# Six of eleven inner tiles of a last projection as block products, with weight sums kept in DRAM

## The chip, the cores and the metric

The kernel runs on one core of a Trainium2 chip. The time is the device time of one execution in microseconds (us). A core has five engines with instruction queues of their own: TensorE (PE in the profile, with PEld for its weight loads), VectorE (DVE), ScalarE (ACT), GpSimd (POOL) and SyncE (SP), which here only issues transfers. Data are worked on in SBUF, a memory of 128 partitions; TensorE writes its sums to PSUM, and everything else lies in DRAM (HBM).

## The reference, cut to what matters

One block of a streaming encoder on 512 tokens of 1,024 features: a normalised input, one combined projection, attention (A) and a gated recurrence (B) side by side, both merged into `h`, then a gated feed-forward part and a last normalisation.

```python
h = h + (g_a * ya + g_b * yb) @ w_o[l]
hn = rmsnorm(h, norm_ffn_g[l])
gu = hn @ w_ffn_in[l]                       # 1024 -> 2 x 2816
g, up = jnp.split(gu, 2, axis=-1)
h = h + (jax.nn.silu(g) * up) @ w_ffn_out[l]   # 2816 -> 1024: the last projection
...
return rmsnorm(h, final_norm_g)
```

The change is about the last projection: 512 tokens x 2,816 inner values x 1,024 outputs, all in float32.

## The kernel before, in words

**Precision.** Each float32 operand is split into a high part (ACT copies it to a shorter float type, line 82) and a low part (DVE subtracts the high part from the source, line 83). A product is then three matmuls (`mm3`, lines 76 to 78): high x high, high x low, low x high. Each loads one 128x128 block of the stationary operand and streams the other past it, 512 or 256 columns at a time.

**Order of stages.** Projections for the recurrence; the first head's queries and keys; the values of the first half of the heads (`v_tile`, line 643); the recurrence's output (`yb`, lines 742 to 747); sixteen heads of attention; its output (`ya`); `w_o` with the sum `h`; the feed-forward's input projection (`fg`, `fu`, lines 842 to 909); the last projection (lines 915 to 987).

**The planner.** The code is laid out by a planner that puts each engine's instructions in an order by its own estimate of when their inputs are ready. Inside `tc.manual_schedule(engines=...)` the named engines keep the order of the code. Before, this holds for PE in the attention heads, not in the last projection. Tiles come from pools: a tag has a number of slots (`bufs`), and an instruction that writes a new tile waits until the slot's earlier tile has been read for the last time. Pools on the left and the right of SBUF open and close in turn, and a new pool's tiles wait for the old tiles below them.

**Weights.** `plan` lists the weight chunks, `load` (line 140) issues their transfers from SP into `raw` tiles (three in the small pool `wp`), `prefetch` (line 220) splits them into `whl` tiles (four in `wp`), and `weights(name, ahead)` asks for a chunk and for the ones behind it.

**The input projection** already works with block products: for `fg` and `fu` from tile 2 on, weights and input are seen as 2x2 blocks, sums of weight blocks are built on DVE (`weight_sums`, line 164), and seven products of sums replace eight of blocks (`block_product`, line 277). The eleven activation tiles `act2[0..10]` (128 x 2 x 512: 256 inner values each, that is two inner tiles of 128 in the matmul's terms) lie in the pool `acp` of 13 slots.

**The last projection before.** The 22 inner blocks of 128 are taken in six chunks of four (`fo0_0` and so on), for the first 512 columns and then for the second. `split_act` splits each activation tile, on POOL for tiles 0, 1, 2 and 4 and on DVE for the rest. For the first half each chunk is applied to the four token tiles (128 tokens) in four PSUM tiles. For the second half four chunks go that way, and the last two are applied token tile by token tile, so that `h_out` (add to `h`, sum of squares, factor), `out_norm`, `h_norm` and the stores of one tile run beside the matmuls of the next. The last token tile is taken in two pieces of 256 columns, in all its chunks. The first half's `h_out` runs when that half is done, with the factor on POOL.

Of the kernel before, what the change touches and what calls it, by code (L numbers as in the profile page):

```python
# [14 lines left out]
P = 128  # L15
# [21 lines left out]
def block_kernel(ctx: ExitStack, tc: tile.TileContext, x, norm_mix_g, w_in, b_merge, rel_table,  # L37
# [700 lines left out]

    for t in range(NT):
        v_tile(0, t)  # L740

    for j in range(KT):
        if j == 6:
            prob = scores(0)
        po = mm_tile(f"po_yb{j}")
        project(po, weights(f"yb{j - j % 2}"), j % 2, rnn)
        dve.scalar_tensor_tensor(zB[j], zB[j], 1.0, po[:], ALU.add, ALU.mult)
# [131 lines left out]
    barrier[0] = "fo0_16"  # L879
# [11 lines left out]
    def split_act(i):  # L891
        o = act2[i]
        pl, bufs = (acp, 13) if i == 0 else (ohp, 6) if i < 7 else (op, 4)
        hi = pl.tile([P, 2, S], F32R, tag="act", bufs=bufs, name=f"act_hi{i}")
        lo = acp.tile([P, 2, S], F32R, tag="act", bufs=13, name=f"act_lo{i}")
        act.activation(hi[:], o[:], AF.Copy)  # L896
        (pool if i in (0, 1, 2, 4) else dve).tensor_sub(lo[:], o[:], f(hi[:]))  # L897
        for c in range(2):
            actT[2 * i + c] = (hi[:, c], lo[:, c])
# [16 lines left out]
    ohp = ctx.enter_context(pool_of("act_hi", 6, "right"))  # L916
    op = ctx.enter_context(pool_of("out", 4, "right"))
    for i, name in enumerate(n for n, *_rest in chunks if n.startswith("fo")):
        if i % 4 >= 2:
            extra[name] = op  # L920
    barrier[0] = None
# [3 lines left out]

    def out_tile(t, po, k0, wf, at):
        for k in range(min(4, FT - k0)):
            kk = k0 + k
            mm3(po[:, 0:at.stop - at.start], actT[kk][0][:, t * P:(t + 1) * P], actT[kk][1][:, t * P:(t + 1) * P],
                wf(0, k, at), wf(1, k, at), kk == 0, kk == FT - 1)  # L930
# [30 lines left out]
    ks = list(range(0, FT, 4))  # L961
    late = 4
    for cc, tags in enumerate(("mmmm", "sstmm")):

        pieces = [(t, every) for t in range(NT)] if cc == 0 else [*((t, every) for t in range(3)), (3, slice(0, CW)), (3, slice(CW, S))]
# [47 lines left out]
```

## Time and profile before

| | |
|---|---|
| runs without profiler, median of 3 | 877.0 us (876.93 to 877.12) |
| the profiled execution's own time | 877.08 us |
| its span, first to last instruction | 875.3 us |
| granted TensorE clock, mean | 0.998 |
| transfers | 90.08 MB, mean 103 GB/s |
| largest groups | L76, L77, L78 on `po_out`: 198 matmuls each |
| whl_fo splits on DVE (L83) | 22, 27.8 us |
| whl_fo splits on ACT (L82) | 22, 23.0 us |

The profile is of one execution. Its page gives busy times, the span in 40 slices, the chain of waits that ended last, and groups of instructions by line, engine, operation and tile; "x198 | 72.5, 366 | 0.0" means 198 instructions, 72.5 us busy, 366 ns each on average, and 0.0 us of idle time on their engine just before them, with the releaser behind it. In the timeline a row is start, length, engine, line, operation, tiles, shape and count. Lines L76 to L83 are those of helpers, so groups are told apart by their tiles: `po_out` is the last projection, `p_fu` and `q_fu` the input projection, `yb` the recurrence's output.

### The profile page before, as it was taken

How to read it: one execution, taken by the hardware profiler on the slowest of the kernel's cores; microseconds unless marked ns; L12 is line 12 of the kernel's file. 1: busy time of each engine (PE TensorE's matmuls, PEld its weight loads, DVE VectorE, ACT ScalarE, POOL GpSimd, SP SyncE). 2: the span in 40 equal slices, each digit the busy share in tenths (PEclk: the TensorE clock that was granted, in tenths of full speed). 3: DMA queues.
4: the chain of work that ended last, by engine and by line, in shares of the span. 5: the costliest groups of instructions: out<-in, count | busy, mean ns of one | idle time of the engine just before them, and what ended most of it. 6: DMA issues, size and time to landing. Idle time of an engine off the chain costs nothing.

```text
span 875.3 us, 12954 instructions
## 1 busy us (share of the span) xinstructions
PE 864.5 (99%) x5028; PEld 760.0 (87%) x5028; DVE 545.9 (62%) x850; ACT 479.7 (55%) x830; POOL 104.2 (12%) x138
## 2 busy tenths in 40 slices
PE   8999999999999999999999999999999999999997
PEld 6977887888888888888888889999999999888886
DVE  5786776543646656566557457888887886644203
ACT  6588687531456656566534367565555654823103
POOL 2022221200122222233000000000000001301100
PEclk9999999999999999999999999999999999999999
DMA  8332334323532222242224531433333332453002
GB/s 268 94 90 84 96 95 122 98 92 100 141 113 72 62 76 81 73 121 64 94 96 151 186 97 41 144 100 104 97 116 101 118 101 78 136 171 121 25 1 97
DMA packets 84030, 90.08 MB, mean 103 GB/s; under 512 B 5376, under 2 KB 70512, under 8 KB 83968
## 3 DMA queue, kind: packets, MB, share of 16 engines
q1 hardware_dynamic: 80288, 81.58, 29.9%
q10 hardware_dynamic: 3680, 7.67, 3.0%
q8 instruction: 39, 0.64, 0.3%
q14 instruction: 23, 0.19, 0.1%
HBM read 87.10 MB, written 2.14 MB: 102 GB/s over the span
## 4 chain that ended last, share of the span: by engine, by line
PE 97%; ACT 1%; DVE 1%; DMA 0%; issue 0%; ACTq 0%
PE po_out L76 5%; PE po_out L78 5%; PE po_out L77 5%; PE p_fg L76 2%; PE o L713 2%; PE p_fg L77 2%; PE p_fg L78 2%; PE p_fu L78 2%; PE p_fu L77 2%; PE p_fu L76 2%; PE pT L693 2%; PE po_gb L77 2%; PE po_gb L76 2%; PE po_ga L76 2%; PE po_v L76 2%; PE po_ga L78 2%
## 5 line engine op out<-in xcount | busy, mean ns | idle before, releaser
L77 PE MATMUL po_out<-whl_fo,act_hi 128*128 128x512 f32 (+1 forms) x198 | 72.5, 366 | 0.0
L76 PE MATMUL po_out<-whl_fo,act_hi 128*128 128x512 f32 (+1 forms) x198 | 72.3, 366 | 0.0
L78 PE MATMUL po_out<-whl_fo,act_lo 128*128 128x512 f32 (+1 forms) x198 | 71.7, 365 | 0.0
L682 POOL TENSOR_SCALAR p<-p,rl 128x128 f32<-128x128 f32 (+1 forms) x64 | 39.6, 637 | 164.5 <-DVE rl L680 164.4
L83 DVE TENSOR_TENSOR whl_fo<-raw_fo,whl_fo 128x1024 fp32r<-128x1024 f32 x22 | 27.8, 1273 | 44.3 <-ACT whl_fo L82 43.9
L82 ACT ACTIVATE whl_fo<-raw_fo 128x1024 fp32r<-128x1024 f32 x22 | 23.0, 1057 | 49.0 <-PE po_out L78 36.8
L897 POOL TENSOR_TENSOR act_lo<-act,act_hi 128x1024 fp32r<-128x1024 f32 x4 | 10.9, 2716 | 323.5 <-ACT act_hi L896 321.4
L679 ACT ACTIVATE p<-p,m 128x128 f32<-128x128 f32 (+1 forms) x64 | 35.8, 562 | 12.7 <-DVE m L678 12.7
L78 PEld LDWEIGHTS po_out<-whl_fo,act_lo 128*128 128x128 f32 x198 | 37.3, 189 | 6.0
L77 PEld LDWEIGHTS po_out<-whl_fo,act_hi 128*128 128x128 f32 x198 | 37.4, 189 | 6.0
L76 PEld LDWEIGHTS po_out<-whl_fo,act_hi 128*128 128x128 f32 x198 | 37.4, 189 | 6.0
L83 DVE TENSOR_TENSOR pp<-pT,pp 128x384 fp32r<-128x384 f32 (+1 forms) x48 | 27.8, 595 | 9.8 <-ACT pp L82 9.7
L678 DVE CUSTOM_DVE_ANT_0 p<-s,bias 128x128 f32<-128x128 f32 (+1 forms) x64 | 29.2, 482 | 3.9 <-PE s L675 3.8
L83 DVE TENSOR_TENSOR whl_qk<-raw_qk,whl_qk 128x1024 fp32r<-128x1024 f32 x16 | 21.5, 1346 | 14.4 <-ACT whl_qk L82 14.3
L76 PE MATMUL po_gr<-xnT,whl_gr 128*128 128x512 f32 (+1 forms) x80 | 28.1, 352 | 0.1
L77 PE MATMUL po_xr<-xnT,whl_xr 128*128 128x512 f32 (+1 forms) x80 | 27.9, 354 | 0.0
L83 DVE TENSOR_TENSOR whl_fg_s<-s_fg,whl_fg_s 128x1024 fp32r<-128x1024 f32 x20 | 25.6, 1293 | 3.7 <-ACT whl_fg_s L82 3.7
L77 PE MATMUL po_gr<-xnT,whl_gr 128*128 128x512 f32 (+1 forms) x80 | 27.8, 348 | 0.0
L78 PE MATMUL po_gr<-xnT,whl_gr 128*128 128x512 f32 (+1 forms) x80 | 27.5, 348 | 0.0
L78 PE MATMUL po_xr<-xnT,whl_xr 128*128 128x512 f32 (+1 forms) x80 | 27.3, 346 | 0.0
L76 PE MATMUL po_xr<-xnT,whl_xr 128*128 128x512 f32 (+1 forms) x80 | 26.6, 351 | 0.6 <-ACT xnT L365 0.6
L83 DVE TENSOR_TENSOR whl_fu_s<-s_fu,whl_fu_s 128x1024 fp32r<-128x1024 f32 x20 | 24.0, 1220 | 4.5 <-ACT whl_fu_s L82 4.5
(336 smaller groups left out, 2984.5 us busy)
## 6 DMA issues: line engine op xcount, KB each, us to landing
raw_fg<-in_w_ffn_in_dram SPq DMA_DIRECT2D x24, 512.0 KB, 4.5
raw_fu<-in_w_ffn_in_dram SPq DMA_DIRECT2D x22, 512.0 KB, 3.8
raw_fo<-in_w_ffn_out_dram SPq DMA_DIRECT2D x22, 512.0 KB, 4.2
raw_qk<-in_w_in_dram SPq DMA_DIRECT2D x32, 256.0 KB, 3.3
raw_xr<-in_w_in_dram SPq DMA_DIRECT2D x8, 512.0 KB, 4.7
raw_gr<-in_w_in_dram SPq DMA_DIRECT2D x8, 512.0 KB, 3.6
raw_gb<-in_w_in_dram SPq DMA_DIRECT2D x8, 512.0 KB, 3.9
raw_v<-in_w_in_dram SPq DMA_DIRECT2D x8, 512.0 KB, 3.6
```

Of the source, the lines that this page charges most:

```text
L76: pe.matmul(o, sh, mh, start=start, stop=False, skip_group_check=parts)
L77: pe.matmul(o, sh, ml, start=False, stop=False, skip_group_check=parts)
L78: pe.matmul(o, sl, mh, start=False, stop=stop, skip_group_check=parts)
L82: act.activation(hi, src, AF.Copy)
L83: dve.tensor_sub(lo, src, f(hi))
L678: dve.tensor_tensor_reduce(prob[qb][:], scs[qb], bias[:, S - w:S], -1.0, 3e38, ALU.add, ALU.min, nmax[:, qb:qb + 1])
L679: act.activation(prob[qb][:], prob[qb][:], AF.Exp, bias=nmax[:, qb:qb + 1], scale=-1.0, accum_out=lsum[:, qb:qb + 1])
L682: pool.tensor_scalar(prob[qb][:], prob[qb][:], rl[:, qb:qb + 1], 1.0, ALU.mult, ALU.mult)
L693: pe.transpose(pt[:, at * P:(at + 1) * P], prob[qb][:, kb * P:(kb + 1) * P], ident[:])
L713: pe.matmul(po[:, S - n:S], st, pp[i][:, part, lo:lo + n], start=kb == 0 and part == 0, stop=kb == NT - 1 and part == 1)
L897: (pool if i in (0, 1, 2, 4) else dve).tensor_sub(lo[:], o[:], f(hi[:]))
```

## The change

Of the eleven inner tiles of 256, tiles 0, 1, 2 (front) and 9, 10 (tail) stay plain, and tiles 3 to 8 form three units of two, (3, 4), (5, 6), (7, 8). A unit is a product of 512 tokens x 512 inner values x 1,024 outputs, seen as 2x2 blocks of 256 tokens x 256 inner values and 256 inner values x 512 outputs, and is worked out with seven block products, for all three units together.

- **Weight sums.** `spill(u)` loads a unit's four weight blocks (512 KB each), forms four sums with four subtractions on DVE, and stores them to DRAM (`sums_d`). It stands ahead of the value tiles (unit 0) and at the first and the fourth `yb` output (units 1 and 2). It uses the four `pt` slots in `aw2` that the attention heads use later for their transposed probabilities (`pp`).
- **Parts.** `fo_part` loads one part (a plain weight block, or a sum out of DRAM), and splits it. There are 31 where there were 22 splits. The first two are asked for at the start of the last pass of the input projection, into the small pool; from there on they rotate over ten `whl` slots (four in `wp`, six in the new pool `op`) and seven raw slots (three and four).
- **Activations.** Front and tail tiles are split whole (tile 0 on POOL, the others on DVE). Of the units, seven half-size parts each are split (`act_part`); `act_sums` and `act_last_sum` form the sums on DVE, four per unit, the last two in place. The pool `op` has eight `act` slots.
- **Order.** The whole stage stands in `manual_schedule` for PE and DVE. All eight quarters (four token tiles x two column halves) have a PSUM tile at once. After the front tiles, five of them are added to `h`; those PSUM tiles then take products, which `read` adds to `h` where one product belongs to more than one quarter. The tail tiles are applied token tile by token tile, first to the left half, then to the right, with `h_out` and `h_norm` in between; only the last token tile's right half is in two pieces of 256 columns, and only for the tail.

The core of the diff:

```diff
-    for cc in range(2):
-        for k0 in range(0, FT, 4):
-            plan(f"fo{cc}_{k0}", cols(w_ffn_out, cc * S, S), rows=k0 * P, kts=min(4, FT - k0))
+    front, units, tail = (0, 1, 2), ((3, 4), (5, 6), (7, 8)), (9, 10)
...
+    def spill(u):
+        r = [aw2.tile([P, 2, S], F32, tag="pt", bufs=4, name=f"spill{u}_{n}") for n in range(4)]
+        for n in range(4):
+            sp.dma_start(out=r[n][:], in_=fo_block(units[u][n // 2], n % 2))
+        b11, b12, b21, b22 = (t[:] for t in r)
+        dve.tensor_sub(b11, b12, b11)
+        dve.tensor_sub(b12, b22, b12)
+        dve.tensor_sub(b22, b22, b11)
+        dve.tensor_sub(b21, b21, b22)
+        for n, i in enumerate((0, 3, 1, 2)):
+            sp.dma_start(out=sums_d[u][n][:], in_=r[i][:])
+
+    spill(0)
     for t in range(NT):
         v_tile(0, t)
+    SPILLS = (0, 3)
     for j in range(KT):
...
+        if j in SPILLS:
+            spill(SPILLS.index(j) + 1)
...
-        pl, bufs = (acp, 13) if i == 0 else (ohp, 6) if i < 7 else (op, 4)
+        pl, bufs = (op, 8) if i in front[1:] else (acp, 13)
...
-        (pool if i in (0, 1, 2, 4) else dve).tensor_sub(lo[:], o[:], f(hi[:]))
+        (pool if i == 0 else dve).tensor_sub(lo[:], o[:], f(hi[:]))
...
+    def fo_part(name, src):
+        raw_pl, bufs = raw_rooms[parts_made[0] % len(raw_rooms)]
+        raw = raw_pl.tile([P, 2, S], F32, tag="raw", bufs=bufs, name=f"raw_{name}")
+        sp.dma_start(out=raw[:], in_=src)
+        pl, tag, bufs = rooms[parts_made[0] % len(rooms)]
+        parts_made[0] += 1
+        hl = pl.tile([P, 2, 2, S], F32R, tag=tag, bufs=bufs, name=f"whl_{name}")
+        split_pair(hl, raw[:])
+        return hl
...
         if j == FT - 2:
             split_act(0)
+            for cc in range(2):
+                fo_plain(0, cc)
...
-    ohp = ctx.enter_context(pool_of("act_hi", 6, "right"))
     op = ctx.enter_context(pool_of("out", 4, "right"))
+    rooms[:] = [(wp, "whl", 4)] * 4 + [(op, "whl", 6)] * 6
+    raw_rooms[:] = [(wp, 3)] * 3 + [(op, 4)] * 4
...
+    def act_sums(u):
+        t = acp.tile([P, 2, 2, 256], F32, tag="act", bufs=13, name=f"s12_{u}")
+        s1, s2 = t[:, 0], t[:, 1]
+        a11, a21, a22 = (part_of(n, u) for n in ("a11", "a21", "a22"))
+        dve.tensor_add(s1, a21, a22)
+        dve.tensor_sub(s2, s1, a11)
+        dve.tensor_sub(a21, a11, a21)
...
+    def make(a, b):
+        for u in range(len(units)):
+            src = ...
+            parts_w[b, u] = fo_part(f"{b}_{u}", src)
+            act_part(a, u)
+
+    def multiply(a, b, half, cc, start):
+        for u in range(len(units)):
+            for i in range(2):
+                x, w = acts[a, u], parts_w[b, u]
+                tok = slice(i * P, (i + 1) * P)
+                for k in range(2):
+                    mm3(quarter[2 * half + i, cc][:], x[:, 0, k, tok], x[:, 1, k, tok], w[:, 0, k], w[:, 1, k],
+                        start and u == 0 and k == 0, u == len(units) - 1 and k == 1, parts=True)
...
+    with tc.manual_schedule(engines={mybir.EngineType.PE, mybir.EngineType.DVE}):
+        split_act(1)
+        fo_plain(1, 0)
+        fo_plain(1, 1)
+        for t, cc in everywhere:
+            plain_tile(front[0], t, cc, True)
+        split_act(2)
+        fo_plain(2, 0)
+        fo_plain(2, 1)
+        for t, cc in everywhere:
+            plain_tile(front[1], t, cc, False)
+        make("a11", "b11")
+        for u in every_unit:
+            act_sums(u)
+        for t, cc in ((2, 0), (3, 0), (0, 1), (1, 1), (3, 1), (0, 0), (1, 0), (2, 1)):
+            plain_tile(front[2], t, cc, False)
+        make("s1", "t1")
+        for t, cc in ((2, 0), (3, 0), (0, 1), (1, 1), (3, 1)):
+            add(t, cc)
+        make("s2", "t2")
+        multiply("a11", "b11", 1, 0, True)
+        read(1, 0, (0, 0))
+        multiply("s1", "t1", 0, 1, True)
+        make("a12", "b21")
+        read(0, 1, (1, 1))
+        for u in every_unit:
+            act_last_sum(u)
+        multiply("s2", "t2", 1, 0, False)
+        make("s3", "t3")
+        read(1, 0, (0, 1))
+        multiply("a12", "b21", 0, 0, False)
+        make("s4", "b22")
+        multiply("s3", "t3", 1, 0, False)
+        read(1, 0, (1, 1))
+        make("a22", "t4")
+        multiply("s4", "b22", 0, 1, False)
+        for i in tail:
+            split_act(i)
+            for cc in range(2):
+                fo_plain(i, cc)
+        multiply("a22", "t4", 1, 0, False)
+        for t in range(NT):
+            for i in tail:
+                plain_tile(i, t, 0, False)
+            h_out(0, t, quarter[t, 0], pool, 0, every)
...
+            for n, (po, at, start) in enumerate(pieces):
+                for i in tail:
+                    plain_tile(i, t, 1, start and i == tail[0], at, po[:, 0:at.stop - at.start])
+                if n == len(pieces) - 1:
+                    part = out_norm(t, n + 1)
+                h_out(1, t, po, dve, n + 1, at)
+            h_norm(t, part, n + 1)
```

More of the change, by code (lines that the diff above doesn't have):

```diff
@@ new lines, in block_kernel, with plain_tile, add @@
+    quarter = {(t, cc): pl.tile([P, S], F32, tag=tag, bufs=bufs, name=f"po_out{t}_{cc}") for (t, cc), (pl, tag, bufs) in c_tags.items()}
+    def plain_tile(i, t, cc, start, at=every, o=None):
+        hi, lo = actT[i]
+        w = plain[i, cc]
+        tok = slice(t * P, (t + 1) * P)
+        for k in range(2):
+            mm3(quarter[t, cc][:] if o is None else o, hi[:, k, tok], lo[:, k, tok], w[:, 0, k, at], w[:, 1, k, at],
+                start and k == 0, k == 1, parts=True)
+    def add(t, cc):
+        hs = ht[t][:, cc * S:(cc + 1) * S]
+        dve.tensor_add(hs, quarter[t, cc][:], hs)
```

86 lines of the change are left out of this document (46 added, 40 removed).

## The prediction

> **What bounds the kernel now.** I read the page first (busy shares, the chain that ended last), then busy time by stretches of the last projection, then PE's timeline there.
>
> ```profile
> span 875.3 us, 12954 instructions
> PE 864.5 (99%) x5028; PEld 760.0 (87%) x5028; DVE 545.9 (62%) x850; ACT 479.7 (55%) x830; POOL 104.2 (12%) x138
> PE 97%; ACT 1%; DVE 1%; DMA 0%; issue 0%; ACTq 0%
> ```
>
> ```profile
> 744.00:805.00 61.00, 61.00 (x287) 51.17 (x287) 29.73 (x26) 28.17 (x31) 8.46 (x3) 1.00 0.42 137
> 805.00:869.00 64.00, 64.00 (x345) 55.46 (x343) 15.53 (x28) 13.28 (x27) 6.02 (x4) 1.00 0.13 44
> ```
>
> Columns of the second view: the stretch and its length, then busy time of PE, PEld, DVE, ACT and POOL, the granted clock, the DMA share and GB/s. PE is busy in every microsecond of the stage that the change rewrites, at clock 1.00, while DVE and ACT are busy for half of its first part and a quarter of its second. The chain is PE for 97%. So a matmul taken out of this stage shortens the time by its step, as long as DVE, ACT and the loads keep up with a faster PE. A busy PE alone is no proof of pace, so the step is taken from start times:
>
> ```profile
> L76 PE MATMUL po_out<-whl_fo,act_hi x198: 277/389/396, 743.8 to 868.5; 128*128 128x512 f32 x154, 128*128 128x256 f32 x44
> L77 PE MATMUL po_out<-whl_fo,act_hi x198: 282/389/398, 744.1 to 868.6; 128*128 128x512 f32 x154, 128*128 128x256 f32 x44
> L78 PE MATMUL po_out<-whl_fo,act_lo x198: 279/389/397, 744.3 to 868.7; 128*128 128x512 f32 x154, 128*128 128x256 f32 x44
> ```
>
> ```profile
> 852.27 0.40 PE L76 MATMUL po_out<-whl_fo,act_hi 128*128 128x512 f32 x1
> ...
> 864.54 0.28 PE L76 MATMUL po_out<-whl_fo,act_hi 128*128 128x256 f32 x1
> ...
> 868.74 0.28 PE L78 MATMUL po_out<-whl_fo,act_lo 128*128 128x256 f32 x1
> ```
>
> The stage has 3 x 154 = 462 wide (512) and 3 x 44 = 132 narrow (256) matmuls. Between the first two timeline rows lie three token tiles of 18 wide ones: (864.54 - 852.27) / 54 = 0.227 us a step. Behind them 36 narrow ones: (868.74 - 864.54) / 35 = 0.120 us. The 389 ns that the view gives for one matmul is a pipelined length, not a step.
>
> **What PE saves.** After the change: the three front tiles are 3 inner tiles x 8 quarters x 2 x 3 = 144 wide matmuls; the seven products, over three units, two token tiles, two k and three parts, are 7 x 36 = 252; the two tail tiles are 84 wide and 24 narrow. Together 480 wide and 24 narrow. By the steps: before 462 x 0.227 + 132 x 0.120 = 120.7; after 480 x 0.227 + 24 x 0.120 = 111.8. PE's work falls by 8.9 us. Of that, about 8.2 (36 x 0.227) is the block product, seven products for eight; the rest is that 108 narrow matmuls become 54 wide ones (0.120 against 0.1135 for half a wide one).
>
> [...]
>
> **What DVE and ACT must now deliver.** Both PE and DVE run the new stage in the order of the code; ACT's order is still planned.
>
> ```profile
> L83 DVE TENSOR_TENSOR whl_fo<-raw_fo,whl_fo 128x1024 fp32r<-128x1024 f32 x20 | 25.3, 1278 | 43.7 <-ACT whl_fo L82 43.3
> L82 ACT ACTIVATE whl_fo<-raw_fo 128x1024 fp32r<-128x1024 f32 x20 | 20.9, 1058 | 49.0 <-PE po_out L78 36.8 <-DMA raw_fo<-in_w_ffn_out_dram 11.2 <-PE q_fu L78 1.0
> L936 DVE TENSOR_TENSOR h<-po_out,h 128x512 f32<-128x512 f32 (+1 forms) x8 | 5.1, 653 | 26.5 <-PE po_out L78 26.5
> ```
>
> ```profile
> 699.79 2.36 DVE L83 TENSOR_TENSOR whl_fg_s<-s_fg,whl_fg_s 128x1024 fp32r<-128x1024 f32 x2 [0.52 <-ACT whl_fg_s L82]
> 702.07 0.69 DVE L178 TENSOR_TENSOR s_fu<-raw_fu,raw_fu 128x512 f32<-128x512 f32 x1
> ...
> 703.27 0.68 DVE L179 TENSOR_TENSOR s_fu<-s_fu,raw_fu 128x512 f32<-128x512 f32 x1
> 733.39 0.62 ACT L82 ACTIVATE whl_fu_a<-raw_fu 128x512 fp32r<-128x512 f32 x1
> ```
>
> Back to back, DVE's step is (702.07 - 699.79) / 2 = 1.14 us at 1,024 elements and (703.27 - 702.07) / 2 = 0.60 at 512. The weight splits rise from 22 to 31, and the activations of the six inner tiles are now split as 21 half-size parts, with 18 half-size sums ahead (nine in act_sums, three in act_last_sum) and in all 13 added reads of PSUM (five adds, eight reads) at about 0.65.
>
> A product takes PE 36 x 0.227 = 8.2 us. Between the end of the first product and the end of the seventh lie 49 us. In them DVE has four reads (8 x 0.65 = 5.2), the last sums (3 x 0.60 = 1.8), four makes of three weight parts and three activation parts (12 x (1.14 + 0.60) = 20.9) and the tail's two activations and four plain parts (6 x 1.14 = 6.8): 34.7 us, 71% of the time. Ahead of the first product the three front tiles give 3 x 48 x 0.227 = 32.7 us; DVE needs there two activations, four plain parts, two makes, nine sums and five adds: 6 x 1.14 + 6 x 1.74 + 9 x 0.60 + 5 x 0.65 = 25.9. Each DVE read waits for a product, and what is queued behind it is the make for the product after next; that has one whole product, 8.2 us, as cover, and needs 1.3 for the read and 1.7 for its first unit. The tile rings fit: of the parts made behind a read, two units take slots that an earlier product has left, and the third waits for the first unit of the product then running, 2.7 us. ACT has about 1.06 + 0.62 for each 1.74 of DVE and runs ahead. I put these at nothing; if the cover were gone, the price is the slower rival's below.
>
> Loads: 31 of 512 KB where there were 22. In steady state three per 8.2 us are 193 GB/s.
>
> ```profile
> 765.00:785.00 20.00, 20.00 (x90) 16.57 (x89) 11.31 (x10) 6.09 (x6) 0.00 (x0) 1.00 0.55 179
> raw_fo<-in_w_ffn_out_dram SPq DMA_DIRECT2D x22, 512.0 KB, 4.2
> ```
>
> 179 GB/s took a DMA share of 0.55 in that stretch, so 193 is an estimated 0.6; with seven raw buffers a load has over one product to land in, against 4.2 us. Nothing.
>
> **The join with the stage before.** Now the planner fills the end of the input projection with matmuls of the last one; in the new order it may not.
>
> ```profile
> 743.83 0.40 PE L76 MATMUL po_out<-whl_fo,act_hi 128*128 128x512 f32 x1
> 745.22 0.28 PE L76 MATMUL p_fu<-bt,whl_fu_s 128*128 128x256 f32 x1
> 751.48 0.28 PE L78 MATMUL p_fu<-bt,whl_fu_a 128*128 128x256 f32 x1
> 741.87 0.38 ACT L285 ACTIVATE keepa_fu<-p_fu 128x256 f32<-128x256 f32 x1 [0.95 <-PE p_fu L78]
> 730.97 1.22 DVE L83 TENSOR_TENSOR whl_fu_s<-s_fu,whl_fu_s 128x1024 fp32r<-128x1024 f32 x1
> ```
>
> Between the first and the third row PE spends 751.60 - 743.83 = 7.8 us, of which 36 are narrow products of the last pair (36 x 0.120 = 4.3); 3.5 us are po_out filling. Without the fillers the last products follow each other. The third product of `fu20` (s3) could start at 743.8: its copy ends at 742.3 and its weights at 732.2. The same plain order of products covers each ScalarE copy (0.38) by a product of 12 x 0.120 = 1.4 us, so the loss lies between 0 and 3.5; below nothing it can't be, since PE has no idle time there. The same bounds hold for a second edit: fo_plain(0, 0) and (0, 1) are now asked for ahead of the last pair's sums and hold two of the four `whl` slots of the small pool, so the last group waits for an earlier one of its own pair; its weights are 13 us early now (732.2 against 745.2), against one split of 1.06 + 1.22. I take 0.5 for both, near the lower end, by the two margins.
>
> **The spill.** Twelve loads, twelve subtractions (12 x 1.14 = 13.7 us of DVE) and twelve stores of 512 KB are added between the value projection and the first attention head, on SP's and DVE's queues.
>
> ```profile
> 163.00:189.00 26.00, 26.00 (x118) 21.65 (x118) 10.43 (x18) 12.43 (x21) 3.65 (x4) 1.00 0.19 61
> 189.00:234.50 45.50, 45.50 (x208) 37.77 (x207) 19.71 (x23) 12.87 (x15) 2.20 (x5) 1.00 0.44 129
> 212.56 1.23 DVE L83 TENSOR_TENSOR whl_yb<-raw_yb,whl_yb 128x1024 fp32r<-128x1024 f32 x1 [0.41 <-ACT whl_yb L82]
> 222.34 0.69 DVE L747 SCALAR_TENSOR_TENSOR zb<-zb,po_yb 128x512 f32<-128x512 f32 x1 [0.40 <-PE po_yb L78]
> 235.15 1.15 DVE L83 TENSOR_TENSOR pp<-pT,pp 128x512 fp32r<-128x512 f32 x2
> out_dram<-h SPq DMA_DIRECT2D x4, 320.0 KB, 2.6
> ```
>
> DVE is free for 71.5 - 30.1 = 41 us of this stretch, so the 13.7 fit. Queued behind a store that waits for its subtraction, or a load that waits for a `pt` slot, are the loads of `yb` on SP; behind a subtraction that waits for its load, the splits of `yb` on DVE. PE needs the last `yb` pair when the sixth output is done (222.3); its last split ends at 213.8, so 8 us are spare. One spill is about four loads at 193 GB/s (2.1 MB: 10.9 us), 4.6 of DVE, four stores (10.9): 26 us, or 11 if the transfers of a spill run side by side (4.2 + 4.6 + 2.6). Three are 34 to 79 us from about 163 on. They share four slots with the first head's `pp`, wanted at 235 and by PE after 48 more wide matmuls (10.9 us) of the second pair, so at 246: 83 us on. Even the upper end fits. I take 0, with 0 to 4 as a bound (half of the 8 spare).
>
> **The end.** Now the first half of the columns is closed long before; after the change it is closed just before the second, for each token tile.
>
> ```profile
> 864.74 0.69 DVE L936 TENSOR_TENSOR h<-po_out,h 128x512 f32<-128x512 f32 x1 [1.00 <-PE po_out L78]
> 867.24 0.55 DVE L957 TENSOR_SCALAR h<-h,ors 128x640 f32<-128x640 f32 x1
> 869.05 0.42 DVE L936 TENSOR_TENSOR h<-po_out,h 128x256 f32<-128x256 f32 x1 [0.24 <-PE po_out L78]
> ```
>
> The third token tile ends 12 wide and 24 narrow steps (5.6 us) before PE's last matmul; its scaling on DVE ends 3.05 us after its add, so 2.3 us before that matmul starts. Then come the add of the last tile's first half (0.65), two narrow pieces with their squares between: I count DVE's last add 0.5 us behind the last matmul's start, against 0.31 now (869.05 - 868.74). 0.2 us more, 0 to 0.9.
>
> **Sum,** against the profiled execution's own 877.08 us (span 875.3; the runs' median, 877.0, is 0.1 below): 877.1 - 8.9 + 0.5 + 0.2 = 868.9 us.
>
> **Rivals.**
> (a) Smaller gain: waits at joins. The planner put the 3.5 us of fillers there, which speaks for it; that none of the inputs is late by the rows, against. With all of them lost, and up to another 2 us where a make's third unit is late, 871 to 874.5; middle 872.
> (b) The spill holds up PE. One spill's 26 us in front of a `yb` load, less 8 spare, is up to 18; with loads only partly behind it 4 to 12: 873 to 881. For it: SP and DVE take their queues in order. Against: both are half idle there.
> (c) Slower: DVE becomes the bound of the products. If the slots leave ACT no room to run ahead, ACT and DVE alternate: a weight part is 1.06 + 1.22, an activation part 0.62 + 0.68, so a make is 10.7 instead of 5.2. The 49 us then hold 5.2 + 1.8 + 4 x 10.7 + 6 x 2.28 = 63.5; the last part is wanted 18 wide steps (4.1) into the tail, so PE is late by 63.5 - 49 - 4.1 = 10.4: 879 us. It decides once DVE needs over 49 + 4 us where I count 35, half as much again. For it: 43.7 us of DVE's idle time is now spent waiting for ACT's half. Against: that ACT itself was then waiting for PE to free weights (36.8), with DVE idle.
> (d) A removed wide matmul is worth less than its step, because the weight loads and not the columns set PE's pace: then it is worth a narrow step, 0.120, and the 36 save 4.3 instead of 8.2: 872.8. For it: PEld is 87% busy. Against: a wide step is 1.9 times a narrow one, as the columns would have it. [...]
>
> **How the numbers follow.** Forecast 0.58, its own range 867.9 to 870.8 (the terms at their low ends give 868.2, less 0.3 for the spread of the runs, 876.93 to 877.12, and a planner that lays out the earlier stages anew; with 2.4 of the join's 3.5 it is 870.8). (a) 0.23, (b) 0.08, (c) 0.09, (d) 0.02. 867.9 to 874.5 holds the forecast, (a), (d) and a little of (b): 0.83. Differences under 0.2% (1.8 us) can't be told from none here. Faster: all of forecast, (a), (d) and a third of (b), 0.86; same: the part of (b) around 877, 0.04; slower: (c) and the end of (b), 0.10.
>
> **What would show it.** Right: po_out with 480 wide and 24 narrow matmuls at the same two steps; PE without idle time in the last 120 us; DVE waiting for PE in the reads, not PE for DVE; `yb` ending where it ended, near 234. Wrong: PE idle before a product with a weight or activation part of DVE as releaser (c); idle before po_yb or a later start of the first head (b); idle in the last products of the input projection or the first of po_out (a); a step unlike 0.227 (d).

## The result, and the profile after

The new kernel takes 869.17 us (median of runs from 868.98 to 869.43) against 877.05 (876.93 to 877.12) for the kernel before on the same chip: a ratio of 0.9911, with an interval of 0.9893 to 0.9928. The forecast was 868.9. The profiled execution took 869.43 us.

The page of the new kernel: span, busy time by engine, the chain that ended last by engine, and the transfers that are new (count, size, microseconds to landing).

```profile
span 867.6 us, 12923 instructions
PE 855.7 (99%) x4938; PEld 750.3 (86%) x4938; DVE 593.1 (68%) x914; ACT 495.0 (57%) x854; POOL 96.8 (11%) x135
PE 86%; DVE 5%; ACT 5%; issue 2%; DMA 2%; POOL 0%; SPq 0%; ACTq 0%; POOLq 0%; DVEq 0%
spill<-in_w_ffn_out_dram SPq DMA_DIRECT2D x12, 512.0 KB, 4.7
sums<-spill SPq DMA_DIRECT2D x12, 512.0 KB, 3.7
raw_t<-sums SPq DMA_DIRECT2D x12, 512.0 KB, 4.5
```

Ninety matmuls are gone (5,028 to 4,938) and 8.8 us of PE's busy time with them; DVE works 47 us more. PE is still 99% busy, but its part of the chain fell from 97% to 86%, with DVE and ACT at 5% each: the chain that ends last now passes through them at some places.

Busy time by stretches: the two that hold the spills, then the last projection in two parts (columns as in the prediction).

```profile
163.00:189.00 26.00, 25.70 (x116) 21.12 (x115) 15.61 (x22) 11.61 (x21) 5.00 (x4) 1.00 0.93 323
189.00:234.50 45.50, 45.50 (x206) 37.73 (x205) 27.84 (x30) 12.88 (x15) 2.20 (x5) 1.00 0.75 253
744.00:800.00 56.00, 55.53 (x263) 46.56 (x262) 42.61 (x53) 33.30 (x43) 0.00 (x0) 1.00 0.56 189
800.00:861.00 61.00, 61.00 (x281) 50.87 (x279) 35.74 (x51) 23.75 (x41) 4.99 (x4) 1.00 0.23 78
```

The spills raise the transfers of the first stretch from 61 to 323 GB/s and DVE's work in both by 13.3 us (43.5 against 30.1), and PE is idle for 0.3 us there. In the last projection PE is idle for 0.47 us in 117.

Where the 7.7 us of span came from is read off PE's timeline: the stage's first matmul, the join with the stage before (that stage's last matmul and the one behind it), the first product, and the last matmul.

```profile
744.13 0.40 PE L76 MATMUL po_out<-whl_fo,act_hi 128*128 128x512 f32 x1
...
752.43 0.28 PE L78 MATMUL p_fu<-bt,whl_fu_a 128*128 128x256 f32 x1
753.19 0.50 PE L76 MATMUL po_out<-whl_fo,act_hi 128*128 128x512 f32 x1 [0.47 <-ACT c_u L283]
...
781.90 0.39 PE L76 MATMUL po_out<-whl_b,x_a 128*128 128x512 f32 x1
...
860.81 0.28 PE L78 MATMUL po_last<-whl_fo,act_lo 128*128 128x256 f32 x1
```

And DVE's timeline: an idle stretch of 8 us while the stage before ends, that stage's last instruction (L950), behind which the work on the new stage begins at once, the first part of the second product, the five adds, and the last tile's factor and last add.

```profile
750.29 0.42 DVE L295 TENSOR_TENSOR c_u<-keepb_fu 128x256 f32<-128x256 f32 x1 [7.96 <-ACT keepb_fu L283]
...
753.16 1.23 DVE L950 TENSOR_TENSOR act<-act,c_u 128x1024 f32<-128x1024 f32 x1 [1.16 <-ACT c_u L283]
...
774.08 1.22 DVE L83 TENSOR_TENSOR whl_t<-raw_t,whl_t 128x1024 fp32r<-128x1024 f32 x1
...
779.29 3.08 DVE L1007 TENSOR_TENSOR h<-po_out,h 128x512 f32<-128x512 f32 x5
...
860.70 0.77 DVE L972 TENSOR_TENSOR h<-h,g_fin 128x256 f32<-128x256 f32 x1 [0.58 <-ACT oj L971]
...
861.63 0.42 DVE L969 TENSOR_TENSOR h<-po_last,h 128x256 f32<-128x256 f32 x1
```

| place | before | after | difference |
|---|---|---|---|
| start of the stage's first matmul | 743.83 | 744.13 | +0.30 |
| from there to the last matmul's start | 124.91 | 116.68 | -8.23 |
| in that, new idle time (waiting for the copy `c_u`) | 0 | 0.47 | +0.47 |
| from the last matmul to DVE's last add | 0.31 | 0.82 | +0.51 |
| from that add to the end of the span | 6.25 | 5.97 | -0.28 |
| sum, without the third row, which is part of the second | 875.3 | 867.6 | -7.7 |

Matmuls alone give 8.23 + 0.47 = 8.70 us, where the prediction worked out 8.9.

The row of the five adds in DVE's timeline is the one to keep in mind. The five adds free the PSUM tiles that the products write; the first product starts into the tile that the first add frees. The adds run back to back from 779.29, and PE starts the product at 781.90, straight behind its front tiles and without a wait. In the experiments where PE does wait for that add, it starts 0.83 us after the adds begin. So it could have started at 780.12 here: the spare time was 1.8 us.

### The profile page after: what moved, and what is told of

Read it like the earlier page. It is cut to its first block, busy times and chain, and to the rows that moved or that the text cites. A ratio compares the mean times of both kernels' runs of the same rounds, so it can differ in the third digit from the quotient of the medians.

```text
span 867.6 us, 12923 instructions
## 1 busy us (share of the span) xinstructions
PE 855.7 (99%) x4938; PEld 750.3 (86%) x4938; DVE 593.1 (68%) x914; ACT 495.0 (57%) x854; POOL 96.8 (11%) x135
## 4 chain that ended last, share of the span: by engine, by line
PE 86%; DVE 5%; ACT 5%; issue 2%; DMA 2%; POOL 0%; SPq 0%; ACTq 0%; POOLq 0%; DVEq 0%
PE po_out L76 4%; PE po_out L78 4%; PE po_out L77 4%; PE p_fg L76 2%; PE o L711 2%; PE p_fu L78 2%; PE p_fg L78 2%; PE p_fu L77 2%; PE p_fg L77 2%; PE p_fu L76 2%; PE pT L691 2%; PE po_ga L76 2%; PE po_ga L78 2%; PE po_ya L76 2%; PE po_h L78 2%
## 5 line engine op out<-in xcount | busy, mean ns | idle before, releaser
L917 POOL TENSOR_TENSOR act_lo<-act,act_hi 128x1024 fp32r<-128x1024 f32 x1 | 2.4, 2417 | 298.6 <-ACT act_hi L916 298.6
L76 PE MATMUL po_out<-whl_fo,act_hi 128*128 128x512 f32 (+1 forms) x80 | 30.8, 385 | 0.5 <-ACT c_u L283 0.5
L78 PE MATMUL po_out<-whl_fo,act_lo 128*128 128x512 f32 (+1 forms) x80 | 30.7, 384 | 0.0
L77 PE MATMUL po_out<-whl_fo,act_hi 128*128 128x512 f32 (+1 forms) x80 | 30.7, 384 | 0.0
L676 DVE CUSTOM_DVE_ANT_0 p<-s,bias 128x128 f32<-128x128 f32 (+1 forms) x64 | 29.2, 483 | 1.8 <-PE s L673 1.8
L82 ACT ACTIVATE whl_fg_s<-s_fg 128x1024 fp32r<-128x1024 f32 x20 | 20.9, 1054 | 10.4 <-PE q_fg L78 5.5
L82 ACT ACTIVATE whl_qk<-raw_qk 128x1024 fp32r<-128x1024 f32 x16 | 16.8, 1051 | 16.2 <-PE po_yb L78 8.8
L76 PE MATMUL po_gb<-xnT,whl_gb 128*128 128x512 f32 x64 | 25.2, 393 | 0.3 <-DVE sp_p L455 0.3
L76 PE MATMUL po_ga<-xnT,whl_ga 128*128 128x512 f32 x64 | 25.3, 395 | 0.0
L77 PE MATMUL po_gb<-xnT,whl_gb 128*128 128x512 f32 x64 | 25.3, 395 | 0.0
```

Source lines behind the costliest of these rows:

```text
L76: pe.matmul(o, sh, mh, start=start, stop=False, skip_group_check=parts)
L77: pe.matmul(o, sh, ml, start=False, stop=False, skip_group_check=parts)
L78: pe.matmul(o, sl, mh, start=False, stop=stop, skip_group_check=parts)
L82: act.activation(hi, src, AF.Copy)
L676: dve.tensor_tensor_reduce(prob[qb][:], scs[qb], bias[:, S - w:S], -1.0, 3e38, ALU.add, ALU.min, nmax[:, qb:qb + 1])
L917: (pool if i == 0 else dve).tensor_sub(lo[:], o[:], f(hi[:]))
```

## Experiments: is each term what the prediction said?

**The spill alone**, on the kernel before: the three calls of `spill` are added, and nothing reads the sums.

```diff
+    spill(0)
     for t in range(NT):
         v_tile(0, t)
+    SPILLS = (0, 3)
...
+        if j in SPILLS:
+            spill(SPILLS.index(j) + 1)
```

> The kernel before with the three spills added at the same places and the sums left unused; the last projection is the old one. Theory (the spill is hidden but for one DVE wait ahead of a value tile, 0.3 us in the trace of after): 877.3 us, 877.0 to 877.7, and one idle stretch of PE near 178 us. Rival (the spill costs more, and the block products give back what it takes): 878.5 us or more, with idle time of PE before po_yb or before the first head.

Measured: 876.67 us (876.55 to 877.64), ratio 0.9999 (0.999 to 1.0008). The expected idle stretch did not come: PE is busy for all of the 26 us from 163 to 189. The 0.3 us there are in the trace of the new kernel alone, so that the spill costs them is not shown.

**The new kernel without the spill.** The `t` parts are loaded from plain blocks of the weights.

```diff
-    spill(0)
...
-        if j in SPILLS:
-            spill(SPILLS.index(j) + 1)
...
-src = ... else sums_d[u]["t1 t2 t3 t4".split().index(b)][:]
+src = ... else fo_block(units[u][int(b[1]) % 2], int(b[1]) // 3)
```

> The kernel after without the spills: the parts t1 to t4 are loaded as plain weight blocks, so the weight sums are left out; all other work stays. Theory: 869.2 less 0.3, 868.9 us (868.5 to 869.3), since the sums cost only the one wait. Rival (17 MB of added traffic slow the core elsewhere too, or the reads of sums from DRAM come late): 867.5 us or less.

Measured: 869.12 us (868.99 to 869.3), ratio 0.9911 (0.9896 to 0.9926), 0.05 below the new kernel. From both sides the spill costs nothing that can be measured, as forecast, though in the new kernel it fills the transfer engines to a share of 0.93 for 26 us.

**The narrow matmuls alone**, on the kernel before: 96 of its 132 narrow ones become 48 wide ones, by taking the last token tile in two pieces in the last two chunks only.

```diff
-    for cc, tags in enumerate(("mmmm", "sstmm")):
+    for cc, tags in enumerate(("mmmm", "sstt")):
...
-        pieces = ... if cc == 0 else [..., (3, slice(0, CW)), (3, slice(CW, S))]
+        pieces = [(t, every) for t in range(NT)]
...
+    hs = ht[3][:, S:]
+    dve.tensor_add(hs, pos[3][:], hs)
+    pieces[3:] = [(3, slice(0, CW)), (3, slice(CW, S))]
+    pos[3:] = [mm_tile(f"po_out1_{i}") for i in (3, 4)]
```

> The kernel before, where only the last two chunks of the last token tile's second half are in pieces of 256 columns: 96 narrow matmuls become 48 wide ones, one add to h is new. Theory (a narrow step is 0.120 and a wide one 0.227): 96 x 0.120 - 48 x 0.227 = 0.6 us less, 876.4 us (876.1 to 876.8). Rival (the term is nothing: PE's start times mislead, or the new add costs as much): 877.0 us.

Measured: 876.34 us (876.11 to 877.12), ratio 0.9993 (0.9984 to 1.0002). The median is 0.7 us lower, the size expected, but the interval just takes in no change. What is left of PE's saving, about eight of nine microseconds, is put down to the block product by its 36 matmuls and their step; no run has that part alone.

## Experiments: how much room does DVE have?

The prediction put every new duty of DVE at nothing, with a margin of half as much work again. Two kernels add work to DVE without touching anything else.

**Low parts of the activations twice:** 21 more DVE instructions of 0.60 us.

```diff
         split_pair(o, src)
+        dve.tensor_sub(o[:, 1], src, f(o[:, 0]))
         acts[name, u] = o
```

> The kernel after, where DVE forms the low part of each of the 21 activation parts of the units twice (same result). That is 21 x 0.60 = 12.7 us more of DVE, against 20 us in which the trace of after shows DVE waiting for PE between 763 and 842 us. Theory (DVE is hidden with a margin): 869.2 us, 868.9 to 869.9. Rival (DVE is as good as the bound, each addition shows): 872 us or more.

Measured: 872.67 us (871.85 to 875.24), ratio 0.9954 (0.9938 to 0.997); the profiled span is 871.4, so 3.8 longer. PE's timeline of this kernel from the first product on,

```profile
783.99 0.47 PE L76 MATMUL po_out<-whl_b,x_a 128*128 128x512 f32 x1 [2.08 <-DVE h L1007]
784.29 0.39 PE L77 MATMUL po_out<-whl_b,x_a 128*128 128x512 f32 x1
784.52 0.59 PE L78 MATMUL po_out<-whl_b,x_a 128*128 128x512 f32 x1
784.91 0.63 PE L76 MATMUL po_out<-whl_b,x_a 128*128 128x512 f32 x1
785.34 0.63 PE L77 MATMUL po_out<-whl_b,x_a 128*128 128x512 f32 x1
...
787.90 0.43 PE L77 MATMUL po_out<-whl_b,x_a 128*128 128x512 f32 x1
788.16 0.39 PE L78 MATMUL po_out<-whl_b,x_a 128*128 128x512 f32 x1
```

and DVE's at the adds:

```profile
783.16 1.28 DVE L1007 TENSOR_TENSOR h<-po_out,h 128x512 f32<-128x512 f32 x2
```

The time is the rival's, but not for its reason: only part of the additions shows. Apart from the 0.47 at the join, PE waits at one place in the stage, 2.08 us, for the first add. Six of the extra instructions stand ahead of it, and it comes 3.9 us later (783.16 against 779.29); less the 1.8 that were spare, that is the wait. The other fifteen, 15 x 0.60 = 9 us behind it, make PE wait nowhere. So among the products the margin held at least 9 us more, and ahead of the first one it was small.

The rest of the loss is in the steps. From 784.52 to 787.90 they are about 0.43 us instead of 0.227; the 11 steps from 783.99 to 788.16 take 4.17 us where 2.50 would be usual: 1.7 lost. 2.1 + 1.7 = 3.8, the whole difference.

**Low parts of the activations and of the 21 weight parts of the products twice.**

```diff
-            parts_w[b, u] = fo_part(f"{b}_{u}", src)
+            parts_w[b, u] = fo_part(f"{b}_{u}", src, 2)
```

> As before, with the low parts of the units' 21 weight parts formed twice too: 21 x 1.74 = 36.5 us more of DVE, more than the 20 us of waiting and the 4 us that the last part has to spare. Theory (a margin of about 24 us, then DVE is the bound): 869.2 + 12 = 881 us, 878 to 884, slower than the kernel before, PE waiting for DVE. Rival (PE's stage is limited by something else, DVE's order doesn't matter): under 873 us.

Measured: 891.55 us (891.49 to 891.79), ratio 1.0165 (1.015 to 1.018). PE's waits in this kernel (microseconds in total, times, the longest), and the stretch around the first product:

```profile
PE po_out L76 <- DVE h L1009: 10.3, 1, 10.3
...
PE po_out L76 <- DVE h L1065: 5.6, 1, 5.6
PE po_out L77 <- DVE whl_fo L83: 1.0, 1, 1.0
```

```profile
785.00:795.00 10.00, 2.97 (x7) 2.42 (x8) 9.89 (x13) 0.00 (x0) 0.00 (x0) 0.58 0.36 119
```

With 36.5 us more (21 x 0.60 + 21 x 1.14) the products themselves run out of cover: 5.6 us for a `read` that frees a PSUM tile (L1065), and 1.0 for a part of the tail. But the largest wait, 10.3, is again that for the five adds (L1009). DVE as the bound is real: at this load the change is slower than the kernel before by 14.5 us. It is also 10 us slower than the theory, which took DVE's waits and the end's spare time as one margin of 24 us for the whole stage. The margin is used up place by place: the three waits are 16.9 us, and slow steps behind the two longer ones cost 2.3 and 2.4 more, 21.6 of the 22.1 by which the span grew.

## Experiments: why are the adds so late?

**Six weight slots instead of ten.** The larger pool gives the `whl` parts ten slots; here it adds two, not six.

```diff
-    rooms[:] = [(wp, "whl", 4)] * 4 + [(op, "whl", 6)] * 6
+    rooms[:] = [(wp, "whl", 4)] * 4 + [(op, "whl", 2)] * 2
```

> The kernel after with six whl slots (four and two) in place of ten. Theory (a make needs only the three slots that the product before the running one has left; ACT then runs less far ahead): 869.2 us, 868.9 to 870. Rival (the larger pool is what keeps ACT ahead of DVE; with six slots the two alternate): 872 us or more.

Measured: 875.53 us (874.9 to 877.42), ratio 0.9984 (0.9975 to 0.9993). Most of the gain is gone, so the theory that the size of the pool does not matter fell. DVE's timeline of this kernel shows how, ScalarE's why, and PE's what it costs:

```profile
775.16 0.68 DVE L83 TENSOR_TENSOR x_s<-s,x_s 128x512 fp32r<-128x512 f32 x1
781.50 1.23 DVE L83 TENSOR_TENSOR whl_t<-raw_t,whl_t 128x1024 fp32r<-128x1024 f32 x1 [5.66 <-ACT whl_t L82]
...
784.98 1.28 DVE L1007 TENSOR_TENSOR h<-po_out,h 128x512 f32<-128x512 f32 x2
```

```profile
780.40 1.06 ACT L82 ACTIVATE whl_t<-raw_t 128x1024 fp32r<-128x1024 f32 x1 [6.47 <-issue]
```

```profile
785.81 0.77 PE L76 MATMUL po_out<-whl_b,x_a 128*128 128x512 f32 x1 [4.13 <-DVE h L1007]
786.38 0.63 PE L77 MATMUL po_out<-whl_b,x_a 128*128 128x512 f32 x1
...
791.86 0.40 PE L78 MATMUL po_out<-whl_b,x_a 128*128 128x512 f32 x1
```

The trace names no releaser for ScalarE's wait; that it is a slot follows from the order of the slots and the time. DVE does nothing from 775.8 to 781.5. The instruction at the head of its queue splits the second unit's part for the second product. With six slots that part takes the slot of `fo_2_0`, which the front's last tile reads down to the seventh of its eight quarters: six steps (1.4 us) before PE's front ends at 785.81 - 4.13 = 781.68, so until about 780.3. ScalarE's half starts at 780.40, DVE's behind it. The adds, whose inputs are there, are queued behind that. Then 4.13 us of idle time, and 14 steps that take 6.05 us instead of 3.18: 7.0 together, the 6.8 by which the span grew.

**Six slots, and the five adds ahead of that make.** If the place in the queue is the cause, moving five lines should undo the whole loss.

```diff
-        make("s1", "t1")
         for t, cc in ((2, 0), (3, 0), (0, 1), (1, 1), (3, 1)):
             add(t, cc)
+        make("s1", "t1")
```

> The new kernel with six weight slots instead of ten, and the five adds of finished quarters put ahead of make(s1, t1) in the written order. Theory: six slots cost 6.4 us only because the adds stand on DVE behind a make that waits for slots. With the adds ahead of it the 4.1 us of idle time of PE before the first product and the lowered clock behind it go: 869.2 (868.9 to 869.9). Rival, six slots are too few for the products themselves (each make then waits for the product before it): 872 or more, with idle time of PE before the second to fourth product.

Measured: 869.16 us (869.08 to 869.29), ratio 0.991 (0.9894 to 0.9927). DVE's and PE's timelines of this kernel:

```profile
774.11 1.88 DVE L1007 TENSOR_TENSOR h<-po_out,h 128x512 f32<-128x512 f32 x3
...
778.33 1.22 DVE L83 TENSOR_TENSOR whl_t<-raw_t,whl_t 128x1024 fp32r<-128x1024 f32 x1
779.47 0.69 DVE L83 TENSOR_TENSOR x_s<-s,x_s 128x512 fp32r<-128x512 f32 x1
781.59 1.23 DVE L83 TENSOR_TENSOR whl_t<-raw_t,whl_t 128x1024 fp32r<-128x1024 f32 x1 [1.43 <-ACT whl_t L82]
```

```profile
781.38 0.39 PE L78 MATMUL po_out<-whl_fo,act_lo 128*128 128x512 f32 x1
781.61 0.39 PE L76 MATMUL po_out<-whl_b,x_a 128*128 128x512 f32 x1
```

The first add now begins at 774.11, 7.5 us ahead of the first product, where it was 2.6 in the new kernel. DVE still waits for ScalarE's halves behind them (1.43 us in the last row), and PE waits nowhere in the stage but for the 0.47 us at the join. Six slots are enough for the products; in the new kernel the four others only cover the place of the adds in the written order.

**The planner's order.** The last stage without `manual_schedule`, so that PE's and DVE's order is planned as it was before the change.

```diff
-    with tc.manual_schedule(engines={mybir.EngineType.PE, mybir.EngineType.DVE}):
-        split_act(1)
+    if True:
+        split_act(1)
```

> The kernel after without the written order: the planner orders PE and DVE in the last projection, as it does elsewhere. Theory (PE's work is the bound and the order only has to keep DVE ahead): 868.5 to 871 us. Rival (the written order is what makes the block products pay, since the planner puts reads and splits in an order that holds up PE): 873 us or more.

Measured: 868.12 us (868.09 to 868.4), ratio 0.9897 (0.9881 to 0.9914): 1.05 below the written order, and the ranges don't meet. In DVE's timeline the first of the five adds stands among the splits, 4.4 us earlier than in the written order:

```profile
774.86 0.69 DVE L1007 TENSOR_TENSOR h<-po_out,h 128x512 f32<-128x512 f32 x1
```

There is no idle time of PE in the stage, and the last add stands 0.63 us behind the last matmul (860.61 against 859.98) instead of 0.82. So 0.47 at the join and 0.19 at the end are placed; the rest of the 1.05 is not. The planner also uses DVE's idle stretch before the join: from 742.61 to 747.3 three sums of activations and one weight split of the new stage stand there, where the written order has nothing.

## Experiments: how far does it go?

**Four units and one front tile**, order written by hand. Tiles 1 and 2 become a unit; twelve wide matmuls fewer, 2.7 us. The cover ahead of the first product shrinks from three plain tiles to one, and the sum s2 is formed in place.

```diff
-    front, units, tail = (0, 1, 2), ((3, 4), (5, 6), (7, 8)), (9, 10)
+    front, units, tail = (0,), ((1, 2), (3, 4), (5, 6), (7, 8)), (9, 10)
...
+        for t, cc in ((2, 0), (3, 0), (0, 1), (1, 1), (3, 1), (0, 0), (1, 0), (2, 1)):
+            plain_tile(front[0], t, cc, True)
         make("a11", "b11")
+        for t, cc in ((2, 0), (3, 0), (0, 1), (1, 1), (3, 1)):
+            add(t, cc)
```

> The kernel after with a fourth unit: tiles 1 and 2 as block products too, one front tile, four spills (at the value tiles and the first, third and fifth yb output), five adds right behind the first make, s2 in place of a11, the first read ahead of the third make. Theory (PE's step is what counts, DVE has 8.3 us of work in each product of 10.9): 12 wide steps less, 869.2 - 2.7 = 866.5 us, up to 867.5 with a wait at a join. Rival (with one front tile DVE has 10.9 us of lead in place of 32.7 and becomes the bound): 870 to 877 us, PE idle before the second and third product with DVE as releaser.

Measured: 876.6 us (875.56 to 878.54), ratio 0.9997 (0.9988 to 1.0006). All of the gain is gone. PE's wait ahead of the first product, the stretch that follows, and ScalarE's timeline ahead of it:

```profile
PE po_out L76 <- DVE h L1007: 8.4, 1, 8.4
```

```profile
765.00:775.00 10.00, 7.24 (x20) 5.77 (x21) 9.64 (x15) 8.77 (x11) 0.00 (x0) 0.58 0.34 129
```

```profile
761.81 1.06 ACT L82 ACTIVATE whl_b<-raw_b 128x1024 fp32r<-128x1024 f32 x1 [2.33 <-DMA raw_b<-in_w_ffn_out_dram]
764.10 1.06 ACT L82 ACTIVATE whl_b<-raw_b 128x1024 fp32r<-128x1024 f32 x1 [1.24 <-DMA raw_b<-in_w_ffn_out_dram]
```

The rival's time came, but with the idle time before the first product and not the second or third. The adds stand behind the first product's make, and two things hold that up. Its raw weights land late (ScalarE waits 2.33 and 1.24 us; DVE, in turn, 3.35 in that make). And all of it but one weight split stands behind the stage before: 33 matmuls of the front tile are now put between that stage's last products (18 in the new kernel), so DVE's last instruction there starts at 756.36 and not at 753.16. How the 8.4 us divide between the two was not measured. The idle time and a granted clock of 0.58 in the stretch shown outweigh the 2.7.

**Four units, planned order.** The same without `manual_schedule`.

> Four units and one front tile as in the run with four units before, but the last stage in the planner's order instead of one written by hand. Twelve wide matmuls fewer are worth 12 x 0.227 = 2.7 us. Theory, it was the written order that put the adds behind late parts: with the planner's order 868.1 - 2.7 = 865.4 (865 to 866.5). Rival, one front tile (10.9 us of PE) is too short a cover in any order, since the parts of the first products must be loaded in it: idle time of PE of 3 us or more before the first or second product, a lowered clock behind it, 869 or more.

Measured: 867.1 us (866.28 to 867.55), ratio 0.9886 (0.9871 to 0.99). PE's one wait in the stage, the stretch in which DVE is fullest, and DVE's first add:

```profile
PE po_out L77 <- DVE whl_b L83: 0.7, 1, 0.7
```

```profile
770.00:800.00 30.00, 30.00 (x134) 24.84 (x133) 30.00 (x35) 22.02 (x28) 0.00 (x0) 1.00 0.83 265
```

```profile
746.37 0.69 DVE L1007 TENSOR_TENSOR h<-po_out,h 128x512 f32<-128x512 f32 x1 [1.57 <-PE po_out L78]
```

The 8.4 us are gone with the order alone: the planner puts the first add at 746.37, as soon as PE has closed its quarter. Neither expectation is quite right: the gain over three planned units is 1.0 and not 2.7, with runs that spread over 1.3 us. 0.7 of the difference is the wait above; the rest has no cause shown. DVE is busy for all of the 30 us shown, so there is little left to give it.

**The end.** DVE's factor at 860.70 in the new kernel stands ahead of the last add. Here the last token tile's first piece takes its factor on POOL, and the last add is moved ahead of the sum of squares.

```diff
-                if n == len(pieces) - 1:
+                if n == len(pieces) - 1 and t < NT - 1:
                     part = out_norm(t, n + 1)
-                h_out(1, t, po, dve, n + 1, at)
+                h_out(1, t, po, dve if t < NT - 1 else pool if n == 0 else None, n + 1, at)
+            if t == NT - 1:
+                part = out_norm(t, n + 1)
+                dve.tensor_mul(ht[t][:, S + CW:], ht[t][:, S + CW:], g_fin[:, S + CW:])
```

> The new kernel with the last token tile's first piece multiplied by the factor on POOL, and the last piece's add ahead of that tile's sum of squares on DVE. Theory: DVE's last add comes 0.82 us after PE's last matmul starts because one factor stands ahead of it; moved away, the add comes at about 0.3 and the end 0.4 to 0.5 earlier: 868.7 (868.4 to 869.0). Rival, what sets the end is the chain of squares and reductions on ACT and DVE whatever order the adds have: 869.2.

Measured: 868.68 us (868.39 to 868.87), ratio 0.9904 (0.989 to 0.9919); 0.49 below the new kernel, and the ranges don't meet. PE's and DVE's timelines:

```profile
860.52 0.28 PE L78 MATMUL po_last<-whl_fo,act_lo 128*128 128x256 f32 x1
```

```profile
860.84 0.42 DVE L969 TENSOR_TENSOR h<-po_last,h 128x256 f32<-128x256 f32 x1 [1.01 <-PE po_last L78]
```

The add follows the last matmul's start by 0.32 us instead of 0.82. Of these 0.5 us 0.4 reach the end in the trace: the span ends 6.4 us behind that start (866.9 - 860.52), where it was 6.8.

**Both together:** four units, planned, with that end.

> Four units and one front tile, the last stage in the planner's order, and at the end the last token tile's first piece multiplied by the factor on POOL with the last add ahead of the sum of squares on DVE: the two edits that gained by themselves, together. If they don't touch each other, 867.1 - 0.5 = 866.6 (866.2 to 867.0). Rival, the planner had already put the last add early, so the second edit brings nothing: 867.1.

Measured: 866.92 us (866.28 to 867.87), ratio 0.9886 (0.987 to 0.9903). DVE's last add comes 0.32 us behind the last matmul's start (858.96 against 858.64), against 0.63 without the edit (859.16 against 858.53), so at most 0.3 was to be had; against a spread of over a microsecond in both kernels it can't be told whether it came. Both are some 10 us below the kernel before and 2 below the change as made.

## Why the prediction was right, and the step that was wrong

**PE's steps: right.** 480 wide and 24 narrow matmuls at the same pace: the products' 252 start from 781.90 on and their last at 838.8 (0.227 a step). 8.7 us were measured for 8.9. Rival (d), a removed wide matmul worth only 0.120 us, would have left 4.3, and the trace does not agree with it.

**The join: right in size, wrong in kind.** 0.47 us of idle time for 0.5, a value picked between 0 and 3.5, so the size is partly luck. The prediction had the fillers gone and the last products following each other. In fact 18 matmuls of the front's first three quarters stand among them (15 before), and the idle time is behind the last product: the fourth quarter's first matmul waits for the last copy, `c_u`, which empties a PSUM tile of the pool that this quarter's tile comes from. Before, and in the planner's order, PE had other matmuls there. The stage's start is 0.30 later besides; the kernel with six slots and early adds, which has the spill too, starts it at 743.84, so that this belongs to the change is not shown.

**The spill, the loads: right.** The spill costs nothing, from both sides, and the last matmul of `yb` starts at 233.6 against 233.2. PE waits for no load in the stage. **The end: right as a sum, by luck:** +0.23 for +0.2. The last add came 0.82 behind the last matmul and not 0.5, and the run with another order shows that it was the factor ahead of it. What follows the last add is 0.28 shorter than before, which no term had.

**DVE's cover: wrong, and it didn't show.** The step that failed is "Ahead of the first product the three front tiles give 3 x 48 x 0.227 = 32.7 us; DVE needs there ... 25.9". The need was nearly right; the cover was not. Busy time in the new kernel from DVE's last instruction on the stage before to the end of the five adds:

```profile
753.16:782.36 29.20, 29.17 (x129) 24.14 (x130) 27.41 (x34) 18.60 (x22) 0.00 (x0) 1.00 0.73 251
```

It is 27.4 us of DVE's work, 1.1 of it that last instruction, and 1.8 of waits. DVE doesn't begin when PE's stage begins. The first work on the stage in its queue splits an activation tile into the new pool `op`, and ScalarE's half of that starts only at 753.14, right behind the last copy of the stage before. What could go earlier, like a weight split whose ScalarE half is done at 745.85, is queued behind it. So DVE begins at 753.16, 9.0 us behind PE's first matmul, and has 28.7 us until 781.90 for 29.2. All five adds are done only at 782.36. That PE didn't wait is luck: only the first add must be done by then, and it was so 1.8 us early, where the prediction has 6.8 for all. The sum of the work was compared with the sum of the time; what had to be compared was the time of one instruction in its queue with the time at which it is wanted. (The "18 half-size sums" of the prediction are 12, nine and three; its sums of time use 12.)

**"The tile rings fit"** is right for ten slots, and for six only with the adds placed earlier. Rival (c) named slots as its condition and the alternation of ACT and DVE as its mechanism; at six slots the loss came, at another place: one instruction waiting for a slot with the adds queued behind it.

**What an idle gap of PE costs** was missing from the rivals' prices. They priced a wait at its length; the runs lost 3.8 us for a gap of 2.08 and 7.0 for one of 4.13.

## What to carry to other kernels

Where an order is written by hand, put ahead in each queue what frees a buffer for the bound engine, and measure the margin at that instruction, from the moment when its engine can start at all. More buffers can hide a bad place in a queue (869.17 us with ten slots, 875.53 with six, 869.16 with six and the adds earlier): before a pool is enlarged, look at what is queued behind the instruction that waits for a slot. If a planner is there, let it order the same code once; in this kernel its order was 1.05 us better for three units and 9.5 better for four.

## What was not expected of the hardware

After the five idle gaps of 2.08 us and more PE ran at about half its pace (0.43 us a step against 0.227) for 4.2 to 6.1 us, in the same instructions.

| idle gap of PE | step after it | slow from the first matmul on | lost in steps |
|---|---|---|---|
| 0.47 us (new kernel) | 0.23 us from the second on | none | 0.1 |
| 0.69 us (four units, planned) | 0.23 us from the second on | none | 0.1 |
| 1.04 us (all low parts twice) | 0.23 us from the second on | none | 0.1 |
| 2.08 us (activations twice) | 0.43 us | 4.2 us | 1.7 |
| 4.13 us (six slots) | 0.43 us | 6.1 us | 2.9 |
| 5.58 us (all low parts twice) | 0.43 us | 5.2 us | 2.4 |
| 8.37 us (four units) | 0.43 us | 5.7 us | 2.7 |
| 10.31 us (all low parts twice) | 0.43 us | 4.8 us | 2.3 |

So among the four gaps from 4.13 to 10.31 us a longer one cost its own length, but not more behind it: 2.3 to 2.9 us.

The granted clock is lowered in the same places. Its means over stretches of 10 us:

| run | first stretch | clock | second stretch | clock |
|---|---|---|---|---|
| activations twice | 775 to 785 | 0.98 | 785 to 795 | 0.85 |
| six slots | 775 to 785 | 1.00 | 785 to 795 | 0.66 |
| four units | 755 to 765 | 0.91 | 765 to 775 | 0.58 |
| all low parts twice, gap of 10.31 us | 785 to 795 | 0.58 | 795 to 805 | 0.91 |
| all low parts twice, gap of 5.58 us | 825 to 835 | 0.80 | 835 to 845 | 0.86 |

The clock within a stretch was not measured. If it is one half where it is lowered, as the steps suggest, the means put the low clock, by estimate, from 784.6 to 788.0, 785.0 to 791.8, 763.2 to 773.4, 786.6 to 796.8 and 831.0 to 837.8; the slow steps end at 787.90, 791.86, 773.41, 796.84 and 837.88. By the same estimate the clock falls about 2.7, 3.3, 3.8, 4.9 and 3.9 us after the gap began, in the first run about 0.6 us after PE had started again and in the others before that.

How long a gap has to be is only bracketed: behind 1.04 us the pace was as before (0.23 us from the second step on), behind 2.08 us it was not (0.43 us), and between the two no gap of this stage tells where it begins.
